# Layer-norm sums: the last k-tile enters TensorE's partition sums as a term of its own

## The chip, the cores and the metric

The kernel runs on one core of a Trainium2 chip. The metric is the device time of one execution in microseconds (us); lower is better. Shown are the median of several executions and one execution that was profiled.

## The reference, cut to what matters

Four layers, each a token mixer (Fourier, attention, pooling, gMLP) and a gated ConvFFN. Every sub-layer normalises twice: the post-norm of the residual sum and, after it, the modulated norm of the next sub-layer.

```python
def _layer_norm(x, g=None, b=None):
    xf = x.astype(F32)
    mu = jnp.mean(xf, axis=-1, keepdims=True)
    var = jnp.mean(jnp.square(xf - mu), axis=-1, keepdims=True)
    y = (xf - mu) * lax.rsqrt(var + LN_EPS)
...
    x_p = _layer_norm(ALPHA * x_p + m_p[2] * y_p, ln_g[i, 0], ln_b[i, 0])
    x_s = _layer_norm(ALPHA * x_s + m_s[2] * y_s, ln_g[i, 0], ln_b[i, 0])
    h_p = _layer_norm(x_p) * (1 + m_p[4]) + m_p[3]
    h_s = _layer_norm(x_s) * (1 + m_s[4]) + m_s[3]
```

The width is 1024 features; 512 sample tokens and 128 prompt tokens run through the same weights.

## The kernel before, in words

The state `x` lies feature-major in SBUF: 8 k-tiles of 128 features (partitions) by 640 tokens. Work on tokens is cut into two halves, `HALVES` 0 and 1 (256 and 384 tokens) or, in two layers, 2 and 3 (384 and 256). A large product is three float32r matmuls for each k-tile (`mm3`, L189 to L191); TensorE (PE) runs these nearly without a break.

A norm needs, for each token, the mean of the values and of the squares over all features, so over 8 k-tiles and 128 partitions. It is done in these steps:

- `sums_add` (L337 to L351) is called for each k-tile as its values come out, either from `evac` (L452, VectorE adds the scaled product to `x`) in `project` and the pooling `mix`, or from `ln1` (L411, L412) in `boundary`. ScalarE squares the tile (L348, tile `lnt`), GpSimd (POOL) adds the values to a running sum (L349, tile `tmp`), and the squares are added to a second running sum (L355) one call later: on POOL where the first norm's sums are built in `project`, on VectorE (DVE) in `boundary` and in `mix`.
- `ln_stats` (L359) adds the last squares on DVE (L355) and has PE sum over the partitions: one float32 matmul of 128x1 for each block of 128 tokens and each of the two sums (L368, tile `st`), with the running sum as the stationary operand and a column of 1/1024 (`onesD`). Then L372 to L376 make the mean and the reciprocal deviation (`lnv`; the power is POOL's), PE broadcasts both over the partitions (L388, tile `bc`), and `centre`, `ln1` and `ln2` (L399, L411, L420) apply them.

`boundary` does this twice for each half. The steps of the first half are handed out between the matmuls of the second (`LN_A`). Those of the second half, the exposed one, lie between the first matmuls of the next stage (`LN_B`, `LN_P`), which run on the first half alone: float32 matmuls (L503) or float32r ones. A scheduler then fixes one instruction order for each engine; engines run in order and wait on semaphores.

There are 30 calls of `ln_stats`, and 150 matmuls of L368.

Of the kernel before, what the change touches and what calls it, by code (L numbers as in the profile page):

```python
# [17 lines left out]
NK = 8  # L18
# [80 lines left out]
def at(d, key):  # L99
    return d.get(key, d[None])  # L100


def steps(g, n):
    for _ in range(n):
        next(g, None)
# [10 lines left out]
class Kern:  # L116
# [206 lines left out]
        return self.mod[L][:, ch, kt, g:g + 1]  # L323


    def sums_new(self, half):

        w = HALVES[half][1] - HALVES[half][0]
        S = types.SimpleNamespace(first=None, last=None, pool=True, nt=w // 128, n=0)
        if w <= 256:  # L330
            t = self.tmp([128, 2, w])
            S.s = (t[:, 0], t[:, 1])
        else:
            S.s = (self.tmp([128, w]), self.tmp([128, w]))
        return S

    def sums_add(self, S, z, t=None, scale=None, bias=None, pool=True):  # L337


        nc = self.nc  # L340
        src, kw = (z, {}) if t is None else (t, dict(scale=scale, bias=bias))
        n, S.n = S.n, S.n + 1
        if n == 0:
            nc.scalar.activation(S.s[1], src, AF.Square, **kw)
            S.first, S.pool = z, pool
            return
        sq = self.small("lnt", [128, z.shape[1]], LNT)
        nc.scalar.activation(sq, src, AF.Square, **kw)  # L348
        nc.gpsimd.tensor_add(S.s[0], z, S.s[0] if n > 1 else S.first)  # L349
        self.sums_end(S)  # L350
        S.last = sq  # L351
# [6 lines left out]
    def ln_stats(self, S, half, eps, together):  # L358


        nc, v = self.nc, self.nc.vector
        a, b = HALVES[half]
        S.pool = False
        self.sums_end(S)
        st = self.st([128, 2, 3])
        for q in range(2):
            for t in range(S.nt):
                nc.tensor.matmul(st[:, q, t:t + 1], S.s[q][:, 128 * t:128 * t + 128], self.onesD, start=True, stop=True)  # L368
        cv = self.small("lnv", [128, 2, 3])
        w = self.small("lnw", [128, 3])  # L370
        n = slice(0, S.nt)
        v.tensor_copy(cv[:, 0, n], st[:, 0, n])  # L372
        nc.scalar.activation(w[:, n], st[:, 0, n], AF.Square)
        v.tensor_sub(w[:, n], st[:, 1, n], w[:, n])
        v.tensor_scalar(out=w[:, n], in0=w[:, n], scalar1=0.0, scalar2=eps, op0=ALU.max, op1=ALU.add)
        nc.gpsimd.tensor_tensor(out=cv[:, 1, n], in0=w[:, n], in1=self.mhalf[:, n], op=ALU.pow)  # L376
        yield
        out = []
        for i in range(2):
            if b - a > 256 or not together:  # L380
                ps = self.bc()
            elif i == 0:
                both = self.bc()
                ps = both[:, 0:256]
            else:
                ps = both[:, 256:512]
            for t in range(S.nt):
                nc.tensor.transpose(ps[:, 128 * t:128 * t + 128], cv[:, i, t:t + 1].to_broadcast([128, 128]), self.ident)  # L388
            out.append(ps[:, 0:b - a])
        yield out  # L390
# [65 lines left out]
    def project(self, gs, units, L, ch, after, fill=None, halves=(0, 1)):  # L456

        ws = {}  # L460
        key = L, ch // 3
        keep = at(KEEP, key)
        sched = list(at(LN_A, key))
        for half in halves:
            S = self.sums_new(half)
            first = half == halves[0]
            a, b = HALVES[half]
            for m in (range(NK) if first else range(NK - 1, -1, -1)):
                if first or m < NK - keep:
                    ws[m] = units(m)  # L470
                ps = self.mm([128, b - a])
                n = len(gs)
                for i in range(n):
                    self.mm3(ps, ws[m](i), (gs[i][:, 0, a:b], gs[i][:, 1, a:b]), i == 0, i == n - 1)
                    while not first and sched and sched[0] <= 8 * (NK - 1 - m) + 8 * i / n:
                        steps(ln, 1)
                        sched.pop(0)
                if first and fill is not None:
                    fill()
                self.evac(ps, L, ch, m, half)  # L480
                self.sums_add(S, self.x[:, m, a:b])
            if first:
                ln = after(half, S)
        steps(ln, 99)
        after(half, S)
# [280 lines left out]
    def boundary(self, L, which, box, pre=None):  # L766

        def ln(half, S):


            together = (L, which) == (2, 0)
            st = self.ln_stats(S, half, EPS_POST, together)
            next(st)
            yield
            MU, R = next(st)
            yield
            if L == DEPTH - 1 and which == 1:
                a, b = HALVES[half]
                for k, t in self.centre(MU, half, AHEAD_L):
                    self.ln1(t, R, L, which, half, k)  # L780
                    self.load(self.a["y"][:, k, a:b], self.x[:, k, a:b])
                    yield
                return
            nL, ch = (L, 3) if which == 0 else (L + 1, 0)
            if half in (0, 2):
                if which == 1 and nL == 2:
                    box["hf"] = [self.act([128, 2, T], F32) for _ in range(NK // 2)]
                else:
                    box["h"] = self.new_h()
                    box["h32"] = self.hlp.tile([128, NK, 256], F32, tag="hl", name=self.nm("h32"))  # L790
            S = self.sums_new(half)
            for k, t in self.centre(MU, half, at(AHEAD, (L, which, half))[0]):
                self.ln1(t, R, L, which, half, k, S)
                yield
            st = self.ln_stats(S, half, EPS, together)
            next(st)
            yield
            MU, R = next(st)
            yield
            for k, t in self.centre(MU, half, at(AHEAD, (L, which, half))[1]):  # L800
                self.ln2(t, R, nL, ch, half, k, box)
                yield

        def after(half, S):
            g = ln(half, S)
            if half in (0, 2):
                return g
            sched = list(LN_P if half == 3 else at(LN_B, (L, which)))
            n = 0
            for i, w in enumerate(pre(box) if pre is not None else ()):  # L810
                n += w
                while sched and sched[0][0] <= n:
                    steps(g, sched.pop(0)[1])
            steps(g, 99)
        return after
# [367 lines left out]
    def pool_pre(self, box):  # L1183

        nc, a = self.nc, self.a
        w = [self.raw_unit(a["wpool"][i], [128, 2, 2, 256]) for i in range(2)]
# [22 lines left out]

        def mix(half):  # L1210
            x0, x1 = HALVES[half]
            S = self.sums_new(half)
            for m in range(NK):
                ps = self.mm([128, x1 - x0])
                nc.tensor.matmul(ps, zero[:, 0:128], zero[:, 0:x1 - x0], start=True, stop=False)
                for t in range(5):
                    lo, hi = BAND_RANGE[t]
                    c0, c1 = max(lo, x0), min(hi, x1)
                    if c0 >= c1:
                        continue  # L1220
                    off = 128 * t - 8
                    nc.tensor.matmul(ps[:, c0 - x0:c1 - x0], u[t][:, 128 * m:128 * m + 128],
                                     band[m // 4][:, (m // 2) % 2, BAND_KIND[t], c0 - off:c1 - off], start=False,
                                     stop=(t == 4 or BAND_RANGE[t + 1][0] >= x1))
                self.evac(ps, 2, 2, m, half, gate)
                self.sums_add(S, self.x[:, m, x0:x1], pool=False)
                yield 2
            return S

        box["pool"] = hw, mix  # L1230
        yield from hw((0, 1, 2))
        S = yield from mix(0)
        for _ in self.after[2, 0](0, S):
            yield 2
# [307 lines left out]
```

## Time and profile before

| | |
|---|---|
| median of 3 runs | 2783.2 us (2778.14 to 2785.08) |
| the profiled execution | 2783.77 us |
| its span in the trace | 2782.0 us |
| PE busy | 2705.3 us, 97% of the span |
| DVE, ACT, POOL busy | 77%, 48%, 16% |
| mean granted clock of PE | 0.987 of full |

The span is the time from the first to the last instruction of the profile. A line of the waits view names the engine that waited, the line and tile it waited for, and the total, the count and the longest. In a timeline, a row is a run of like instructions on one engine: start, length, engine, line, operation, output and inputs, and in brackets the idle time before it and who ended it. A float32 matmul leaves more than one record of each kind (PEld is the load of the stationary operand, PE the product).

### The profile page before, as it was taken

What the parts mean: (1) busy time and instruction counts of PE and PEld (TensorE: products, weight loads), DVE (VectorE), ACT (ScalarE), POOL (GpSimd) and SP (SyncE); (2) the same over time, 40 slices, a digit from 0 to 9 for tenths busy, and PEclk for the clock granted to TensorE, in tenths of its full rate; (3) what the DMA queues carried; (4) which work ended last, traced back from release to release, by engine and by line L of the source; (5) the groups of instructions that cost most, each with busy time, mean ns of one, the idle gap of its engine ahead of it and who ended that gap; (6) DMA issues with size and microseconds to landing.
All of it is one profiled execution on the core that took longest, in us unless ns stands there. A gap on an engine that the chain in (4) does not pass through costs nothing. (4 is left out here: it accounts for less than half of the span.)

```text
span 2782.0 us, 46206 instructions
## 1 busy us (share of the span) xinstructions
PE 2705.3 (97%) x17466; PEld 2583.4 (93%) x17466; DVE 2134.0 (77%) x4636; ACT 1345.6 (48%) x2424; POOL 455.2 (16%) x477
## 2 busy tenths in 40 slices
PE   7999999999999999999999999999999999999998
PEld 3799999999989999999978999989689999999998
DVE  6879987786697887777487778876997858776775
ACT  4656232335576662323366544454632237544563
POOL 1251000015312400000253000014200024000013
PEclk9999999999999999999988999999999999999999
DMA  6735655452312344444203345653453323344462
GB/s 234 252 107 172 199 169 156 159 167 80 113 52 77 107 153 159 149 155 160 90 34 106 107 113 153 163 146 116 150 188 123 124 74 114 99 111 117 122 152 70
DMA packets 110880, 367.84 MB, mean 132 GB/s; under 512 B 12609, under 2 KB 15297, under 8 KB 110529
## 3 DMA queue, kind: packets, MB, share of 16 engines
q1 hardware_dynamic: 102016, 341.28, 38.0%
q0 software_dynamic: 8640, 23.60, 4.8%
q8 instruction: 138, 2.26, 0.3%
q14 instruction: 86, 0.70, 0.1%
HBM read 335.73 MB, written 2.88 MB: 122 GB/s over the span
## 5 line engine op out<-in xcount | busy, mean ns | idle before, releaser
L189 PE MATMUL mm<-act,hl 128*128 128x384 f32 (+3 forms) x4448 | 1383.8, 312 | 11.2 <-ACT lnt L720 8.2
L191 PE MATMUL mm<-act,hl 128*128 128x384 f32 (+3 forms) x4448 | 1379.9, 311 | 8.3 <-DMA hl<-raw 4.3
L190 PE MATMUL mm<-act,hl 128*128 128x384 f32 (+3 forms) x4448 | 1379.4, 310 | 2.4 <-POOL act L434 1.6
L189 PEld LDWEIGHTS mm<-act,hl 128*128 128x128 f32 x4448 | 842.2, 189 | 18.6 <-ACT lnt L720 9.9
L191 PEld LDWEIGHTS mm<-act,hl 128*128 128x128 f32 x4448 | 842.0, 189 | 10.9 <-DMA hl<-raw 5.3
L190 PEld LDWEIGHTS mm<-act,hl 128*128 128x128 f32 x4448 | 842.8, 189 | 5.2 <-POOL act L434 2.6
L174 ACT CAST hl<-raw 128x1024 fp32r<-128x1024 f32 (+4 forms) x449 | 432.9, 969 | 447.7 <-PE mm L191 312.0
L299 DVE SCALAR_TENSOR_TENSOR bc<-raw,cbc 128x512 f32<-128x512 f32 x608 | 406.8, 720 | 112.9 <-DMA raw<-in_wmod 112.7
L179 DVE TENSOR_TENSOR hl<-raw,hl 128x1024 fp32r<-128x1024 f32 (+4 forms) x384 | 455.5, 1191 | 45.2 <-ACT hl L174 42.9
L452 DVE SCALAR_TENSOR_TENSOR x<-mm,mod,x 128x256 f32<-128x256 f32 (+2 forms) x456 | 185.2, 435 | 155.5 <-PE mm L191 154.5
L349 POOL TENSOR_TENSOR tmp<-x,tmp 128x256 f32<-128x256 f32 (+1 forms) x180 | 178.5, 996 | 145.7 <-DVE x L452 100.4
L177 POOL DMA_DIRECT2D hl<-raw x60 | 51.9, 864 | 638.0 <-ACT hl L176 389.7
L545 DVE SCALAR_TENSOR_TENSOR tmp<-ap,vecs,tmp 128x512 f32<-128x512 f32 x232 | 112.7, 547 | 48.4 <-ACT tmp L543 48.2
L558 POOL MEMSET ap<- 128x1 f32 x24 | 2.2, 104 | 842.4 <-DVE tmp L545 373.3
L183 ACT CAST act<-tmp 128x640 fp32r<-128x640 f32 (+1 forms) x125 | 88.8, 710 | 94.5 <-DVE tmp L550 60.4
L399 DVE TENSOR_TENSOR lnt<-x,bc 128x256 f32<-128x256 f32 (+1 forms) x240 | 110.1, 480 | 13.0 <-PE bc L388 12.8
L547 ACT ACTIVATE tmp<-tmp 128x640 f32<-128x640 f32 x58 | 42.9, 740 | 158.2 <-DVE tmp L545 158.2
L348 ACT ACTIVATE lnt<-x 128x256 f32<-128x256 f32 (+1 forms) x112 | 51.2, 466 | 129.4 <-DVE x L452 127.1
L184 DVE TENSOR_TENSOR act<-tmp,act 128x640 fp32r<-128x640 f32 (+1 forms) x125 | 99.9, 799 | 11.0 <-ACT act L183 10.5
L355 DVE TENSOR_TENSOR tmp<-tmp,lnt 128x384 f32<-128x384 f32 (+1 forms) x126 | 94.2, 749 | 13.6 <-ACT lnt L348 12.4
L503 PE MATMUL mm<-h,raw 128*128 128x256 f32 x416 | 101.2, 399 | 1.8 <-DVE lnt L420 1.8
L174 ACT CAST hl<-sums 128x1024 fp32r<-128x1024 f32 x60 | 62.9, 1049 | 77.1 <-PE mm L191 50.8
(267 smaller groups left out, 3687.5 us busy)
## 6 DMA issues: line engine op xcount, KB each, us to landing
raw<-in_wup SPq DMA_DIRECT2D x216, 512.0 KB, 3.6
raw<-in_wmod SPq DMA_DIRECT2D x184, 512.0 KB, 4.0
raw<-in_wdn SPq DMA_DIRECT2D x55, 448.0 KB, 3.7
hl<-raw POOLq DMA_DIRECT2D x30, 512.0 KB, 5.4
raw<-in_wgv SPq DMA_DIRECT2D x24, 512.0 KB, 3.6
raw<-in_wdn SPq DMA_DIRECT2D x23, 512.0 KB, 3.6
raw<-in_wgo SPq DMA_DIRECT2D x19, 512.0 KB, 4.0
raw<-in_wqk SPq DMA_DIRECT2D x18, 512.0 KB, 3.5
```

The costliest lines, as they stand in the source:

```text
L174: nc.scalar.copy(hl[:, 0], r)
L179: (e or nc.vector).tensor_sub(hl[:, 1], r, hl[:, 0])
L184: (e or self.nc.vector).tensor_sub(dst[:, 1], src, dst[:, 0])
L189: t.matmul(out, lhs[0], rhs[0], start=start, stop=False, skip_group_check=on)
L190: t.matmul(out, lhs[0], rhs[1], start=False, stop=False, skip_group_check=on)
L191: t.matmul(out, lhs[1], rhs[0], start=False, stop=stop, skip_group_check=on)
L299: nc.vector.scalar_tensor_tensor(out=self.bc(), in0=r[:, sl], scalar=1.0, in1=self.cbc[:, g, sl], op0=ALU.mult, op1=ALU.mult, accum_out=ac ...
L349: nc.gpsimd.tensor_add(S.s[0], z, S.s[0] if n > 1 else S.first)
L399: self.nc.vector.tensor_sub(t, self.x[:, k, a:b], MU)
L452: nc.vector.scalar_tensor_tensor(out=self.x[:, m, s0:s1], in0=ps[:, s0 - a:s1 - a], scalar=sc, in1=self.x[:, m, s0:s1], op0=ALU.mult, op1= ...
L503: self.nc.tensor.matmul(ps, w[:, k, :], h32[:, k, :], start=k == 0, stop=k == NK - 1)
L545: nc.vector.scalar_tensor_tensor(out=c[:, sl], in0=ap[:, o + i:o + i + n], scalar=cw(i), in1=c[:, sl], op0=ALU.mult, op1=ALU.add)
```

## The change: what it does

In 18 of the 30 calls `sums_new` is made with `direct` set: in `project` for halves 1 and 3, in `boundary` for halves 1 and 3 and for both halves of two boundaries, and in the pooling `mix` for both halves. There, the eighth k-tile's values and squares are not added to the running sums. They are kept as `S.tail`, and `ln_stats` issues a second matmul behind each of L368's (L374 in the changed file), with the tail tile as the stationary operand, accumulating into the same column of `st` (L376). The add of the seventh tile's squares stays where it was.

```diff
-    def sums_new(self, half):
+    def sums_new(self, half, direct=False):
...
-        S = types.SimpleNamespace(first=None, last=None, pool=True, nt=w // 128, n=0)
+        S = types.SimpleNamespace(first=None, last=None, pool=True, nt=w // 128, n=0, direct=direct, tail=None)
...
         nc.scalar.activation(sq, src, AF.Square, **kw)
+        if S.direct and n == NK - 1:
+            self.sums_end(S)
+            S.tail = (z, sq)
+            return
         nc.gpsimd.tensor_add(S.s[0], z, S.s[0] if n > 1 else S.first)
...
-                nc.tensor.matmul(st[:, q, t:t + 1], S.s[q][:, 128 * t:128 * t + 128], self.onesD, start=True, stop=True)
+                sl = slice(128 * t, 128 * t + 128)
+                nc.tensor.matmul(st[:, q, t:t + 1], S.s[q][:, sl], self.onesD, start=True, stop=S.tail is None)
+                if S.tail is not None:
+                    nc.tensor.matmul(st[:, q, t:t + 1], S.tail[q][:, sl], self.onesD, start=False, stop=True)
...
-            S = self.sums_new(half)
+            S = self.sums_new(half, half in (1, 3))
...
-            S = self.sums_new(half)
+            S = self.sums_new(half, half in (1, 3) or (L, which) in ((1, 1), (2, 0)))
...
-            S = self.sums_new(half)
+            S = self.sums_new(half, True)
```

The order changes near these calls. On PE, at the second norm of the second half behind layer 0's ConvFFN, at about 695 us of the trace, before:

```order
L191 MATMUL mm_7169<-act_6605,hl_7129 128x256
L368 MATMUL st_7195<-onesD,tmp_6968 128x1 x3
L368 MATMUL st_7195<-onesD,tmp_6969 128x1 x3
L946 MATMUL mm_7209<-onesH,tmp_7161 128x1 x2
L189 MATMUL mm_7221<-act_6598,hl_7166 128x256
```

and in the changed program:

```order
L191 MATMUL mm_7180<-act_6613,hl_7140 128x256
L374 MATMUL st_7205<-onesD,tmp_6980 128x1
L376 MATMUL st_7205<-onesD,x 128x1
L374 MATMUL st_7205<-onesD,tmp_6980 128x1
L376 MATMUL st_7205<-onesD,x 128x1
L374 MATMUL st_7205<-onesD,tmp_6980 128x1
L376 MATMUL st_7205<-onesD,x 128x1
L374 MATMUL st_7205<-onesD,tmp_6981 128x1
L376 MATMUL st_7205<-onesD,lnt_7038 128x1
L374 MATMUL st_7205<-onesD,tmp_6981 128x1
L376 MATMUL st_7205<-onesD,lnt_7038 128x1
...
L954 MATMUL mm_7225<-onesH,tmp_7172 128x1 x2
```

Six matmuls have become twelve, between the same neighbours. On PE, at the second norm of the second half behind the pooling mixer, at about 1504 us, before:

```order
L503 MATMUL mm_15875<-h_15414,raw_15873 128x256 x6
L368 MATMUL st_15846<-onesD,tmp_15712 128x1 x3
L503 MATMUL mm_15875<-h_15414,raw_15873 128x256 x2
L368 MATMUL st_15846<-onesD,tmp_15713 128x1 x3
L503 MATMUL mm_15892<-h_15414,raw_15890 128x256 x7
L388 MATMUL bc_15900<-identr,lnv_15853 128x128 x3
```

and in the changed program:

```order
L511 MATMUL mm_15919<-h_15448,raw_15917 128x256 x2
L374 MATMUL st_15884<-onesD,tmp_15752 128x1
L511 MATMUL mm_15919<-h_15448,raw_15917 128x256 x2
L376 MATMUL st_15884<-onesD,x 128x1
L374 MATMUL st_15884<-onesD,tmp_15752 128x1
...
L511 MATMUL mm_15919<-h_15448,raw_15917 128x256
L374 MATMUL st_15884<-onesD,tmp_15753 128x1
L376 MATMUL st_15884<-onesD,lnt_15810 128x1
...
L511 MATMUL mm_15919<-h_15448,raw_15917 128x256 x3
L511 MATMUL mm_15936<-h_15448,raw_15934 128x256 x7
L396 MATMUL bc_15944<-identr,lnv_15897 128x128 x3
```

The first sum stands four wide matmuls earlier, and ten instead of seven wide matmuls stand between them and the broadcast. On POOL, at the program's end (the last k-tiles of half 3), before:

```order
L355 TENSOR_TENSOR tmp_28478<-tmp_28478,lnt_28707 128x256
L349 TENSOR_TENSOR tmp_28478<-x,tmp_28478 128x256
L355 TENSOR_TENSOR tmp_28478<-tmp_28478,lnt_28740 128x256
L349 TENSOR_TENSOR tmp_28478<-x,tmp_28478 128x256
L376 TENSOR_TENSOR lnv_28783<-lnw_28784,mhalf 128x2
```

and in the changed program:

```order
L360 TENSOR_TENSOR tmp_28538<-tmp_28538,lnt_28767 128x256
L354 TENSOR_TENSOR tmp_28538<-x,tmp_28538 128x256
L360 TENSOR_TENSOR tmp_28538<-tmp_28538,lnt_28800 128x256
L384 TENSOR_TENSOR lnv_28845<-lnw_28846,mhalf 128x2
```

POOL's last add of values is gone; its last add of squares stays.

## Rows read from the trace of the kernel before

**Rows 1.** Page, part 1: busy time, share of the span, instructions

```profile
PE 2705.3 (97%) x17466; PEld 2583.4 (93%) x17466; DVE 2134.0 (77%) x4636; ACT 1345.6 (48%) x2424; POOL 455.2 (16%) x477
```

**Rows 2.** Waits of PE: total us, times, longest us

```profile
PE st L368 <- POOL tmp L349: 8.5, 8, 2.2
PE bc L388 <- POOL lnv L376: 8.5, 10, 1.4
PE mm L189 <- ACT lnt L720: 8.2, 6, 2.6
PE mm L191 <- DMA hl<-raw: 4.3, 4, 1.3
PE mm L191 <- DVE hl L179: 4.0, 4, 1.9
PE mm L190 <- DVE hl L179: 3.0, 2, 1.6
...
PE st L368 <- DVE tmp L355: 0.8, 1, 0.8
```

**Rows 3.** Instructions of L368: records, ns min/median/max, then the matmuls' own count

```profile
L368 PEld LDWEIGHTS st<-onesD,tmp x300: 186/192/338, 142.4 to 2770.8; 128*128 128x128 f32 x150
```

**Rows 4.** Timeline near 695 us: start us, length us, engine, line

```profile
694.59 0.28 PE L190 MATMUL mm<-act,hl 128*128 128x256 f32 x1
...
694.71 0.28 PE L191 MATMUL mm<-act,hl 128*128 128x256 f32 x1
694.72 1.43 PEld L368 LDWEIGHTS st<-onesD,tmp 128*128 128x128 f32 x12
694.83 1.40 PE L368 MATMUL st<-onesD,tmp 128*128 128x1 f32 x12
```

**Rows 5.** Timeline near 1439 us, PE's loads

```profile
1439.51 0.93 PEld L368 LDWEIGHTS st<-onesD,tmp 128*128 128x128 f32 x4 [0.91 <-DVE tmp L355]
```

**Rows 6.** Windows in layers 1 and 2: stretch, length, busy, then PEclk, DMA

```profile
1403.00:1407.00 4.00, 1.82 (x17) 1.62 (x15) 3.96 (x9) 2.59 (x5) 3.92 (x4) 1.00 0.00 0
1407.00:1414.00 7.00, 7.00 (x36) 6.92 (x35) 3.37 (x10) 0.59 (x2) 5.47 (x7) 0.51 0.69 246
...
1437.50:1451.00 13.50, 10.73 (x34) 8.29 (x35) 11.61 (x33) 6.80 (x19) 4.62 (x8) 0.51 0.00 0
...
1468.50:1478.50 10.00, 8.19 (x25) 6.62 (x25) 8.50 (x23) 6.22 (x13) 3.08 (x4) 0.50 0.00 0
...
1506.00:1513.00 7.00, 7.00 (x22) 5.75 (x21) 2.70 (x5) 2.52 (x4) 1.70 (x1) 0.52 0.46 154
```

**Rows 7.** Timeline of the last norm, from 2767.9 us

```profile
2767.92 0.73 POOL L349 TENSOR_TENSOR tmp<-x,tmp 128x256 f32<-128x256 f32 x1
...
2768.26 0.61 DVE L452 SCALAR_TENSOR_TENSOR x<-mm,mod,x 128x128 f32<-128x128 f32 x2 [1.91 <-PE mm L191]
2768.60 0.73 POOL L355 TENSOR_TENSOR tmp<-tmp,lnt 128x256 f32<-128x256 f32 x1
2768.99 0.42 ACT L348 ACTIVATE lnt<-x 128x256 f32<-128x256 f32 x1 [2.12 <-DVE x L452]
2769.28 0.73 POOL L349 TENSOR_TENSOR tmp<-x,tmp 128x256 f32<-128x256 f32 x1
2769.50 0.79 DVE L355 TENSOR_TENSOR tmp<-tmp,lnt 128x256 f32<-128x256 f32 x1 [0.63 <-ACT lnt L348]
...
2770.07 1.05 PE L368 MATMUL st<-onesD,tmp 128*128 128x1 f32 x8 [1.85 <-POOL tmp L349]
```

**Rows 8.** Timeline near 1504 us, second norm behind the pooling mixer

```profile
1501.19 1.07 POOL L349 TENSOR_TENSOR tmp<-x,tmp 128x384 f32<-128x384 f32 x1 [0.20 <-ACT x L412]
...
1501.97 0.71 ACT L412 ACTIVATE x<-lnt,vecs 128x384 f32<-128x384 f32 x1
...
1502.82 1.38 POOL L349 TENSOR_TENSOR tmp<-x,tmp 128x384 f32<-128x384 f32 x1 [0.56 <-ACT x L412]
...
1504.25 0.83 PE L368 MATMUL st<-onesD,tmp 128*128 128x1 f32 x6 [2.22 <-POOL tmp L349]
```

## The prediction

> **What bounds the kernel now.** I read the page's busy times first: PE is busy 2705 of 2782 us, no other engine over 77% [rows 1]. So what PE has to do is nearly the whole time, and anything added to PE costs its length unless it falls into one of PE's waits. Second the waits of PE, to see what this change could win. PE waits for the sums' inputs 8.5 us for POOL's adds of values and 0.8 us for DVE's adds of squares, in nine waits, the longest 2.2 us; it waits another 8.5 us before the broadcasts, for POOL's power [rows 2]. Third the timelines around the norms, to see what one more sum costs PE and what ends its wait: most of the 18 changed calls look like the one at 695 us, with no wait at all before the sums [rows 4], and a few like those at 1504 and 2770 us, where PE stands 2.22 and 1.85 us for POOL [rows 7, 8]. Last the windows for PE's granted clock, since the sums of layers 1 and 2 lie partly where it is 0.50 to 0.52, the 1.2 GHz level [rows 6].
>
> **What is removed.** 18 adds on POOL and 18 on DVE, 0.73 to 1.38 us each in the rows that show one [rows 7, 8]. Neither engine sets the pace, so they are worth only what PE waits for them: at most 9.3 us [rows 2].
>
> **What is added.** Of the 18 calls, 13 work on 384 tokens (three blocks, two sums: 6 more matmuls) and 5 on 256 (4 more): 78 + 20 = 98 matmuls on PE. Their price stands in the trace. Each of L368's 150 matmuls left two records (300) [rows 3], and in a group the records follow each other at the pace of the loads: 12 loads take 1.43 us, the last of them 0.19, so a step is (1.43 - 0.19) / 11 = 0.113 us, though the product has one column. That is nearly what a 256-column float32r product costs beside it (694.59 to 694.71, 0.12 us) [rows 4]. So one matmul costs PE 2 x 0.113 = 0.225 us, and 98 of them **22.1 us**. The bounds: 98 x 0.119 x 2 = 23.3 if the whole 1.43 us is divided by 12, and 11 us if each matmul stood alone behind a wide one, whose product hides the first of its two loads, as the load that starts at 694.72 lies under the product of 694.71 [rows 4]. In the new order nearly all stand in groups of 6 to 12; some nine are alone between wide matmuls, which takes back 9 x 0.113 = **1.0 us**.
>
> The Trainium skill (FP8 and Floating Point Precision, TensorE Precision Notes) says that true FP32 takes four passes through the array. The trace has two records for each such matmul [rows 3]; if four were paid at a record's price, the added work would be 44 us instead of 22 and the sum 22 us higher. The records, whose time is measured, decide.
>
> At the 1.2 GHz level four loads took 0.93 us, 0.23 each, against 1.43 / 12 = 0.12 [rows 4, 5]. About 16 of the 98 lie in the half-clock windows (both second norms and the pooling mixer's first one) [rows 6]; at 0.11 us more for each of two records, 16 x 2 x 0.11 = **3.5 us** more.
>
> **What comes back.** The wait before the sums goes only as far as the next input is early. At the program's end the last values are in `x` at 2768.87 (2768.26 + 0.61), and the sixth add of values ends at 2768.65; the first sum may start at about 2768.95 instead of 2770.07, 1.1 us of the 1.85 [rows 7]. Late next is POOL's add of squares that stays, which ends at 2769.33, and ScalarE's last square, at 2769.41; four matmuls on the values keep PE until 2769.85, so these cost nothing. The sums then end at 2768.95 + 8 x 0.225 = 2770.75, against 2771.12: the last norm gains 0.4 us net. DVE's add of squares (2769.50 to 2770.29) was already beneath PE's four records on the values. Near 1504 us, `x` is written at 1502.68 (1501.97 + 0.71) and POOL's last remaining add ends at 1502.26, so the sum of values may start at about 1502.75: 1.5 us earlier [rows 8]. But it now takes 12 records where it took 6, and the second sum still waits for DVE's remaining add of squares. Together 2.6 of 4.07 us, 64%; applied to the 9.3 us [rows 2], **5.9 us** come back. The bounds are 0, if the remaining adds are as late, and 9.3.
>
> Behind the sums, the wait for POOL's power (8.5 us, 10 times [rows 2]) begins when the sums end and moves with them; the work between them does not get shorter. The new order puts a wide matmul or more beneath some of these waits. I take **2 us** back, bounds 0 and 5.
>
> New waits: each tail matmul waits for ScalarE's last value or square, and wide matmuls stand behind it in PE's queue. In the first norm these come from `evac` and were waited for anyway (POOL's and DVE's adds needed the same tiles), so no new one is counted. DVE's 18 adds less free it a little earlier for the splits of L179, for which PE waits 7 us elsewhere [rows 2], mostly not near a norm; I take nothing.
>
> **The sum.** 22.1 - 1.0 + 3.5 - 5.9 - 2 = +16.7 us on the profiled execution's 2783.8, so 2800.5. That execution lies 0.6 us above the median of the runs; against the median I forecast **2800 us**, 0.6% slower. With the unknowns at their ends the sum runs from about 7 (11 + 3.5 - 5.9 - 2) to 27 (23.3 + 3.5): 2790 to 2811.
>
> **Rivals.** *The added work is absorbed later.* In parts of layers 2 and 3 other engines hold PE up: ScalarE's L720, the DMA into `hl` and DVE's splits, 19.5 us together [rows 2]. If those engines' work does not move with PE's lateness, PE meets these waits late and they shrink. For it: the waits are there. Against it: ScalarE and DVE work there on what PE produces, so they are late with it. If half is absorbed, +16.7 - 10 = +7: 2790.
>
> *The added products cost less than their loads.* The first load of a group is hidden beneath the product ahead of it [rows 4]; if half of the loads were, the added work is at its lower bound of 11 us and the sum +16.7 - 11 + 1.0 = +7 as well: 2790. Against it: eleven steps of 0.113 us in a row [rows 4]. The Trainium skill (TensorE: Matmul & The Clock Gate, Wait — 56ns, not 53.3ns?) says that starts of small products come no closer than about 25 ns; whoever takes that floor for the price gets, as an estimate, 196 x 0.025 = 4.9 us and no change in the time. The trace agrees that it is a floor, and shows that this group does not reach it.
>
> *The waits were worth more than their length: faster.* The clock falls to the 1.2 GHz level right after PE's waits of 2.18 and 2.22 us (PE busy 1.82 of 4.00 us before 1407, at 1.00; then 0.51) [rows 6, 8]. If, with the last adds gone, PE does not stand still there, the clock may stay at 2.4 GHz in all four windows: 7 + 13.5 + 10 + 7 = 37.5 us at half pace, 19 us won. With all of the 9.3 and of the 8.5 us back: 22.1 - 1.0 - 9.3 - 8.5 - 19 = -16: 2768. It decides when more than 21 us come back. Against it: the two waits shrink by about two thirds at best, what fills them has one column, and 11 of the 18 calls have neither a wait nor a low clock to lose.
>
> *The clock falls at more places.* Each added group keeps PE on one-column products for up to 1.4 us longer. If four of the norms at 1.00 fell to half for 7 us as in rows 6, each would cost 3.5 us: 2814. Against it: the 12 records at 695 us already run at full pace [rows 4].
>
> That the change doesn't do what it says I leave out: the order shows the doubled matmuls and the missing adds.
>
> **How the numbers follow.** The forecast 0.66, absorbed 0.12, cheap products 0.05, faster 0.07, clock lower 0.10. A measurement of this kernel tells about 0.3%, 8.4 us, from no change. Faster by more takes the case of the waits alone, 0.07; within 0.3% lie the absorbed case and the cheap products, 0.17; slower is the forecast and the lower clock, 0.76. The range takes in the forecast's bounds, most of the two cases within 0.3% and a part of the lower clock: 2787 to 2812. It leaves out the faster case, the low ends of those two and the high end of the last.
>
> **What would show it.** PE's busy time up by 15 to 25 us. The records of L374 and L376 together 496 (300 + 196), stepping at 0.113 us in groups. The wait for POOL before the sums down from 8.5 to 3 to 5 us, not gone. The norm at 695 us longer by 1.3 us with nothing behind it shorter. At the end the sums start some 1.1 us earlier after the last product and the tail gains under 0.5 us. I would be wrong if the group's step were far from 0.113 us, if the low-clock windows vanished, or if PE's waits in layers 2 and 3 fell by 10 us.

## The result and the profile after

The changed kernel takes 2798.9 us (median of 6 runs, 2793.9 to 2808.9) against 2781.4 us for the kernel before (6 runs beside it): a ratio of 1.0072 [1.0057, 1.0088], slower by 20 us [16, 24]. Repeated (`after_again` below) it was 1.0054 [1.0039, 1.0069], 15 us [11, 19]. The forecast was 2800 us, or +16.7 us on the profiled execution.

The profiled execution of the changed kernel took 2793.94 us, the shortest of its six; its span of 2792.2 us is only 10.2 us longer than that of before, at the same mean granted clock of 0.987. One execution is not the mean of many: a second profile of the unchanged kernel (`control` below) has PE busy 2697.0 us at 0.989, where the first has 2705.3 us at 0.987. The readings below say which part of the 15 to 20 us this one shows and which it does not.

The page's busy times, which answer to [rows 1]:

```profile
PE 2727.8 (98%) x17662; PEld 2606.4 (93%) x17662; DVE 2116.0 (76%) x4618; ACT 1345.0 (48%) x2424; POOL 434.8 (16%) x459
```

PE is busy 22.5 us longer and has 196 more records: 98 matmuls of two each. POOL and DVE have 18 instructions less each. PE's idle time (span less busy) goes from 76.7 to 64.4 us.

The records of the two lines of sums (engine, operation, count; ns min/median/max; first and last start in us), for [rows 3]:

```profile
L374 PE MATMUL st<-onesD,tmp x300: 164/250/353, 138.4 to 2781.0; 128*128 128x1 f32 x150
```

```profile
L376 PE MATMUL st<-onesD,x x98: 167/250/352, 177.5 to 2780.3; 128*128 128x1 f32 x98
L376 PE MATMUL st<-onesD,lnt x98: 167/250/352, 179.7 to 2781.2; 128*128 128x1 f32 x98
```

300 + 196 = 496, as forecast. The norm of [rows 4], with the record behind the sums in PE's timeline of before, and then PE's timeline of the changed kernel:

```profile
696.09 0.58 PE L946 MATMUL mm<-onesH,tmp 128*128 128x1 f32 x4
```

```profile
695.32 0.28 PE L191 MATMUL mm<-act,hl 128*128 128x256 f32 x1
695.44 0.28 PE L374 MATMUL st<-onesD,tmp 128*128 128x1 f32 x2
695.58 0.36 PE L376 MATMUL st<-onesD,x 128*128 128x1 f32 x2
695.80 0.36 PE L374 MATMUL st<-onesD,tmp 128*128 128x1 f32 x2
...
697.81 0.36 PE L376 MATMUL st<-onesD,lnt 128*128 128x1 f32 x2
698.04 0.58 PE L954 MATMUL mm<-onesH,tmp 128*128 128x1 f32 x4
```

No wait stands before the sums, and 24 records follow each other: from 695.58 to 697.81, 20 records later, are 2.23 us, 0.112 us each. From the group's start to the next product are 2.60 us, where 12 records took 1.26 (694.83 to 696.09): 1.34 us more, as forecast.

PE's waits, for [rows 2]:

```profile
PE mm L189 <- ACT lnt L728: 7.5, 6, 1.7
PE st L374 <- POOL tmp L354: 5.0, 5, 2.4
PE bc L396 <- POOL lnv L384: 4.0, 6, 1.4
PE mm L190 <- DVE hl L179: 2.6, 2, 1.6
PE mm L191 <- DMA hl<-raw: 2.5, 2, 1.3
PE mm L191 <- DVE hl L179: 2.1, 7, 0.5
...
PE st L374 <- DVE lnw L382: 1.0, 1, 1.0
PE bc L396 <- DVE lnv L380: 0.8, 3, 0.3
```

The waits before the sums fall from 9.3 to 6.0 us, but the longest is still there: 2.4 us. The 1.0 us for L382 is a new wait, for DVE; the waits of before have none of the kind. The waits before the broadcasts fall from 9.3 us (8.5 and, in a row not shown ahead, 0.8 for DVE) to 4.8. Those for L728 (L720 before), for the DMA into `hl` and for DVE's splits fall from 19.5 to 14.7.

**Where the longest wait stayed.** The second norm of layer 1's second sub-layer, PE before, then PE and POOL in the changed kernel:

```profile
1406.62 1.15 PE L368 MATMUL st<-onesD,tmp 128*128 128x1 f32 x6 [2.18 <-POOL tmp L349]
```

```profile
1410.43 0.38 PE L374 MATMUL st<-onesD,tmp 128*128 128x1 f32 x2 [2.36 <-POOL tmp L354]
```

```profile
1409.07 2.00 POOL L354 TENSOR_TENSOR tmp<-x,tmp 128x384 f32<-128x384 f32 x2
```

PE stands for POOL's last remaining add of this half (the first of the two in the row) as long as it stood for the removed one: 2.36 us, against 2.18 before. The order of PE tells why: between the sums ahead of these and these, the trace of before has 133 other product records, that of after 120. The scheduler has put the sums 13 records further forward. At the norm of [rows 8] the sums were put forward too, and the wait falls, but by 1.1 us and not the 1.5 forecast, from 2.22 to 1.13:

```profile
1511.78 0.38 PE L374 MATMUL st<-onesD,tmp 128*128 128x1 f32 x2 [1.13 <-POOL tmp L354]
```

**The end.** The last norm, for [rows 7]:

```profile
2779.42 0.72 POOL L360 TENSOR_TENSOR tmp<-tmp,lnt 128x256 f32<-128x256 f32 x1
```

```profile
2779.52 0.38 PE L374 MATMUL st<-onesD,tmp 128*128 128x1 f32 x2 [0.50 <-POOL tmp L354]
...
2781.10 0.36 PE L376 MATMUL st<-onesD,lnt 128*128 128x1 f32 x2
```

Here no wide product of a next stage stands behind the sums, and the wait falls from 1.85 to 0.50 us. The sums last 16 records instead of 8, 0.9 us more, so that about 0.45 us is gained.

**The clock.** Windows of the changed kernel (stretch, length, then busy of PE, PEld, DVE, ACT, POOL, then PEclk), each pair a stretch with a group of 24 records and the one behind it:

```profile
695.40:698.00 2.60, 2.60 (x26) 2.60 (x24) 0.00 (x0) 0.75 (x2) 1.24 (x1) 1.00 0.04 13
699.50:702.90 3.40, 3.40 (x18) 3.40 (x17) 0.00 (x0) 0.00 (x0) 0.68 (x1) 0.50 0.38 140
963.00:965.80 2.80, 2.80 (x26) 2.80 (x27) 1.13 (x3) 1.49 (x3) 0.00 (x0) 0.99 0.75 293
965.80:969.20 3.40, 3.40 (x19) 3.40 (x18) 2.13 (x4) 1.04 (x1) 0.86 (x1) 0.51 0.82 274
1979.00:1982.90 3.90, 3.90 (x28) 3.12 (x26) 3.90 (x11) 3.90 (x11) 0.00 (x0) 1.00 0.52 150
1982.90:1986.30 3.40, 3.40 (x6) 1.56 (x6) 3.29 (x11) 0.93 (x4) 0.88 (x1) 0.50 0.72 292
2358.00:2361.80 3.80, 3.80 (x36) 3.80 (x34) 2.69 (x3) 2.40 (x4) 0.00 (x0) 1.00 0.73 208
2361.80:2368.60 6.80, 6.80 (x33) 6.80 (x34) 2.93 (x7) 2.26 (x3) 0.86 (x1) 0.50 0.75 263
```

PE is busy all the time and the clock at 1.00 (0.99 in one row) while the group runs; at its end, or up to 1.5 us behind it, the granted clock falls to the 1.2 GHz level for 3.4 or 6.8 us. Two more new stretches begin at 180.7 us, behind groups of 8 and 10 records, and at 1959 us, behind one of 24. In the profile of before the norms at these six places run at 1.00. A fall does not follow every such group: three more groups of 24, at 203, 941 and 2330 us, have none behind them, and in the second profile of the changed kernel (`after_again`) only three of the six places have one (699, 966 and 1983 us). On the other side four stretches of before are gone: the one near 1506 us [rows 6], which `after_again` has again at 1512 us, one of 6.8 us near 769, and two of 3.4 us near 144 and 1864. So this one execution has as low a mean clock as the profiled one of before; over all the timed runs the mean granted clock of the changed kernel was 0.9847 (6 runs) and 0.9858 (5), that of the kernel before 0.9886 in the 21 runs beside the latter.

### The profile page after: what moved, and what is told of

It reads as the page before. It is cut to its first block, busy times and chain, and to the rows that moved or that the text cites. A ratio compares the mean times of both kernels' runs of the same rounds, so it can differ in the third digit from the quotient of the medians.

```text
span 2792.2 us, 46536 instructions
## 1 busy us (share of the span) xinstructions
PE 2727.8 (98%) x17662; PEld 2606.4 (93%) x17662; DVE 2116.0 (76%) x4618; ACT 1345.0 (48%) x2424; POOL 434.8 (16%) x459
## 4 chain that ended last, share of the span: by engine, by line
PE 63%; DVE 3%; issue 2%; ACT 2%; DMA 2%; POOL 1%; SPq 0%; POOLq 0%; ACTq 0%; DVEq 0%
PE mm L189 18%; PE mm L191 17%; PE mm L190 17%; PE mm L1298 1%; PE mm L511 1%; DMA hl<-raw 1%; PE bc L189 1%; PE bc L191 1%; PE bc L190 1%; PE st L374 1%; DMA raw<-in_wup 1%; PE mm L1391 1%; PE st L376 1%; ACT x L420 1%; PE mm L1213 0%
## 5 line engine op out<-in xcount | busy, mean ns | idle before, releaser
L354 POOL TENSOR_TENSOR tmp<-x,tmp 128x256 f32<-128x256 f32 (+1 forms) x162 | 157.7, 978 | 114.3 <-DVE x L460 78.4
L184 DVE TENSOR_TENSOR act<-tmp,act 128x640 fp32r<-128x640 f32 (+1 forms) x125 | 99.8, 798 | 10.2 <-ACT act L183 9.8
L420 ACT ACTIVATE x<-lnt,vecs 128x256 f32<-128x256 f32 (+1 forms) x128 | 82.2, 648 | 23.4 <-DVE lnt L419 22.7
```

The lines of the kernel that those rows point to most:

```text
L420: nc.scalar.activation(z, t, AF.Identity, scale=scale, bias=bias)
```

## The experiments

The theory: each added matmul costs two loads of 0.112 us, part of that is taken out of waits, and the rest is the slowdown. The rivals, as they were put to the runs: the loads are cheap and something else is slow; the falling clock carries most of it; the removed adds are worth a lot (or nothing). Differences in us below are (ratio - 1) x 2777, the kernel before's time beside these runs.

**The kernel before, word for word** (`control`). No edit.

> The kernel before, word for word: what the comparison itself shows of no change. All theories: within 0.1% (3 us).

Ratio 0.9999 [0.999, 1.0008]. Its profile, with a span of 2774.6 us, serves below as a second trace of before:

```profile
PE 2697.0 (97%) x17466; PEld 2577.8 (93%) x17466; DVE 2133.3 (77%) x4636; ACT 1345.2 (48%) x2424; POOL 458.7 (17%) x477
```

**The matmuls without their gain** (`price`). The kernel before, with a second matmul behind each of the 18 calls' sums, which multiplies the running sum by a column of zeros; all adds stay.

```diff
+        self.zeroD = cp.tile([128, 1], F32, name="zeroD")
...
-                nc.tensor.matmul(st[:, q, t:t + 1], S.s[q][:, 128 * t:128 * t + 128], self.onesD, start=True, stop=True)
+                sl = slice(128 * t, 128 * t + 128)
+                nc.tensor.matmul(st[:, q, t:t + 1], S.s[q][:, sl], self.onesD, start=True, stop=not S.direct)
+                if S.direct:
+                    nc.tensor.matmul(st[:, q, t:t + 1], S.s[q][:, sl], self.zeroD, start=False, stop=True)
```

> Before with 98 more partition-sum matmuls at the 18 changed calls, against a column of zeros, and all adds kept: the matmuls alone. Theory A (each added matmul costs PE two loads of 0.113 us, and the long groups let the clock fall at some places): 22 us for the matmuls and 5 to 12 us for the clock, 25 to 33 us slower than before. Rival B (the matmuls hide and the change is slow because PE waits for ScalarE's last tile): under 10 us slower.

1.0091 [1.0076, 1.0106]: +25 us [21, 29], with a mean clock of 0.985. Its page:

```profile
PE 2730.7 (97%) x17662; PEld 2608.4 (93%) x17662; DVE 2134.2 (76%) x4637; ACT 1346.3 (48%) x2424; POOL 456.7 (16%) x477
```

and two pairs of its windows around long groups:

```profile
694.00:697.00 3.00, 3.00 (x28) 3.00 (x28) 0.87 (x5) 0.51 (x3) 0.46 (x2) 1.00 0.12 22
697.00:700.40 3.40, 3.40 (x19) 3.40 (x17) 0.05 (x1) 0.00 (x0) 0.77 (x1) 0.50 0.41 140
939.00:942.80 3.80, 3.80 (x30) 3.67 (x30) 1.87 (x8) 0.47 (x2) 0.00 (x0) 1.00 0.66 259
942.80:946.20 3.40, 3.40 (x13) 2.85 (x12) 1.55 (x4) 1.31 (x2) 0.86 (x1) 0.50 0.35 86
```

So the added matmuls alone make the whole slowdown (15 to 20 us) or more, and they bring falls of the clock with them, with every add kept and the waits for POOL before the sums nearly as they were (8.0 us against 8.5).

**The gain without its matmuls** (`drop`). The changed kernel without the line that keeps the tail: the eighth k-tile is neither added nor multiplied in the 18 calls, so their sums run over seven of eight tiles.

```diff
         if S.direct and n == NK - 1:
             self.sums_end(S)
-            S.tail = (z, sq)
             return
```

> The change without its second matmuls: the last k-tile is left out of both sums at the 18 calls, so only the adds go. Theory A: 4 to 9 us faster than before, from PE's waits before the sums and no further; the waits for POOL before the sums fall below 5 us. Rival C (the adds' waits also cost the clock and the waits behind them): 15 us faster or more, with fewer low-clock windows in layers 1 and 2.

1.0020 [1.0008, 1.0031]: 6 us slower, where 4 to 9 us faster was expected. Its wait for POOL before the sums is not shorter but longer than the control's 8.5 us:

```profile
PE st L373 <- POOL tmp L353: 10.9, 8, 4.9
```

PE's timeline and POOL's at the longest of them:

```profile
2344.31 1.44 PE L373 MATMUL st<-onesD,tmp 128*128 128x1 f32 x6 [4.92 <-POOL tmp L353]
```

```profile
2338.54 5.71 POOL L353 TENSOR_TENSOR tmp<-x,tmp 128x384 f32<-128x384 f32 x4 [0.15 <-ACT x L419]
```

```profile
2341.70:2348.50 6.80, 4.19 (x19) 4.19 (x20) 6.80 (x7) 3.82 (x8) 2.48 (x2) 0.50 0.44 149
```

The same sums in the control start at 2344.63 without a wait, with 193 other product records between them and the sums ahead; here there are 152. The scheduler has moved the sums forward by 41 records, further than the missing add makes POOL early. PE then stands 4.9 us, and the clock falls. This chain is read from the trace; the missing adds under PE's old order were not tried, so how much of the 6 us it makes is open. Over the whole profile PE's idle time is only 1.2 us above the control's, and the mean granted clock of the runs is 0.9881 against 0.9888.

**The same change with 64 equal columns** (`after_wide`). The matmuls of the sums write 64 columns instead of one, all alike; only the first is read.

```diff
-        self.onesD = cp.tile([128, 1], F32, name="onesD")
+        self.onesD = cp.tile([128, 64], F32, name="onesD")
...
-        st = self.st([128, 2, 3])
+        st = self.st([128, 2, 3, 64])
...
```

> The change with the column of 1/1024 widened to 64 equal columns (all sums come out 64 times; column 0 is used). Theory A (steps are paced by the loads, 0.113 us; the clock falls behind the long groups of one-column products): the groups keep their step, the new low-clock places outside the pooling layer vanish, 7 to 13 us slower than before instead of 17. Rival D (the falls belong to the waits, not to the products): 15 to 20 us slower, the same low-clock places. Rival E (64 columns lengthen the step): over 20 us slower, step above 0.113 us.

1.0035 [1.0022, 1.0048]: +10 us, with a mean clock of 0.992. Windows that begin with the same four groups of 24 and reach past them:

```profile
700.40:707.00 6.60, 6.60 (x59) 6.60 (x59) 0.99 (x6) 1.66 (x6) 2.12 (x2) 1.00 0.29 87
964.80:972.00 7.20, 6.51 (x57) 6.29 (x55) 4.87 (x10) 4.61 (x7) 0.76 (x1) 1.00 0.89 300
1978.70:1986.00 7.30, 7.30 (x36) 4.77 (x35) 6.35 (x18) 3.48 (x11) 0.89 (x1) 1.00 0.71 230
2355.60:2366.00 10.40, 8.95 (x76) 8.54 (x75) 8.33 (x16) 6.75 (x13) 0.86 (x1) 1.00 0.71 247
```

Inside the groups the step stays at 0.111 to 0.112 us, so it does not depend on whether the product has 64 columns or one; what is left to set it, as far as these runs show, is the load of each record. But the clock stays at 1.00 behind them. The time is 5 to 10 us below that of the changed kernel. Part of that is the falls, but the wider tile changes the order too: PE is busy 10.9 to 14.6 us less than in the two profiles of the changed kernel and idle some 8 us more.

A count over all fourteen profiles bears the falls out. Taken are groups of sums' records that start at 1.00 and have PE idle for less than 0.5 us from 4 us ahead to the group's end, and a fall counts if it begins between the group's start and 2 us behind its end. Of 25 groups of 24 one-column records 14 have one, of 52 groups of 12 none; of 13 groups of 24 records with 64 columns none.

**The zeros with 64 columns** (`price_wide`). The edit of `price` and that of `after_wide` together.

```diff
+        self.zeroD = cp.tile([128, 64], F32, name="zeroD")
...
-                nc.tensor.matmul(st[:, q, t:t + 1], S.s[q][:, 128 * t:128 * t + 128], self.onesD, start=True, stop=True)
+                sl = slice(128 * t, 128 * t + 128)
+                nc.tensor.matmul(st[:, q, t, :], S.s[q][:, sl], self.onesD, start=True, stop=not S.direct)
+                if S.direct:
+                    nc.tensor.matmul(st[:, q, t, :], S.s[q][:, sl], self.zeroD, start=False, stop=True)
```

> The kernel before with 98 more matmuls against zeros, all with 64 columns. The one-column form of it was 25 us slower than before, the 64-column form without the added matmuls 5.6 us slower. Theory A (22 us are the loads, the rest the clock): 24 to 30 us slower than before with hardly a low-clock window outside the pooling layer. Rival I (much of the 25 us was the clock): under 20 us.

1.0058 [1.0046, 1.007]: +16 us [13, 19]. Its page and the stretch that was at half clock in `price`:

```profile
PE 2719.9 (97%) x17662; PEld 2599.5 (93%) x17662; DVE 2135.5 (76%) x4637; ACT 1346.7 (48%) x2424; POOL 453.7 (16%) x477
```

```profile
697.00:704.00 7.00, 7.00 (x62) 7.00 (x62) 3.52 (x11) 1.63 (x6) 0.86 (x1) 1.00 0.26 76
```

Less than the 24 to 30 us expected, so the rival, that much of the 25 us was the clock, is borne out. PE is busy 10.8 us less than in `price`, and the mean granted clock of the runs is 0.991 against 0.985. Of the 25 us, some 9 are the clock's, if the 64 columns change nothing else; the next run shows that they do.

**The kernel before with 64 columns** (`before_wide`). The edit of `after_wide` on the kernel before.

```diff
-        self.onesD = cp.tile([128, 1], F32, name="onesD")
+        self.onesD = cp.tile([128, 64], F32, name="onesD")
...
```

> The kernel before with the same 64 columns. Theory A: its groups are half as long and follow a wait in most low-clock places, so 0 to 5 us faster, the pooling mixer's low-clock window shorter. Rival D: no change, within 3 us. Rival E: 3 us slower or more.

1.0020 [1.0011, 1.0029]: 6 us slower, where 0 to 5 us faster was expected, and this at a higher mean clock (0.991 against 0.989). Its page, at a span of 2782.5 us:

```profile
PE 2699.3 (97%) x17466; PEld 2576.9 (93%) x17466; DVE 2135.6 (77%) x4636; ACT 1344.7 (48%) x2424; POOL 453.4 (16%) x477
```

PE is idle 83.2 us (span less busy) against 77.6 in the control, and its waits are spread over many lines. Why is open: the wider tile changes the order as well, and that was not taken apart. Against this kernel, `price_wide` has 20.6 us more PE work and 10.4 us less idle time. Against it too, and on the same chip, `after_wide` is 5 us slower (2787.7 against 2782.8): with 64 columns in both kernels the change costs a third or less of what it costs with one.

**Half of the calls each** (`first_only`, `second_only`). The first keeps `direct` in `project` and `mix` alone (48 of the 98 matmuls), the second in `boundary` alone (50).

```diff
-            S = self.sums_new(half, half in (1, 3) or (L, which) in ((1, 1), (2, 0)))
+            S = self.sums_new(half)
```

> The change at the nine calls of the first norms alone (project and the pooling mix): 48 of the 98 matmuls. Theory A (the price is each matmul's loads and the clock behind long groups): 7 to 11 us slower, about half of the change. Rival F (the second norms carry the loss, since their sums lie between matmuls of the next stage, while the first norms' fill a wait): 0 to 4 us slower.

1.0059 [1.0045, 1.0072]: +16 us, above the 7 to 11 expected. Its three groups of 24 records, at 935, 1959 and 2331 us, all have a fall to 0.50 behind them, and the mean granted clock of its runs is 0.9872 against 0.9886 for the kernel before.

```diff
-            S = self.sums_new(half, half in (1, 3))
+            S = self.sums_new(half)
...
-            S = self.sums_new(half, True)
+            S = self.sums_new(half)
```

> The change at the nine calls of the second norms alone (boundary): 50 of the 98 matmuls. Theory A (each matmul costs its loads wherever it stands): 6 to 12 us slower. Rival G (the first norms alone were as slow as the whole change, so the second norms' matmuls fill waits or shorten a chain that PE waits for): within 4 us of before.

1.0043 [1.0026, 1.006]: +12 us, in the range. The two make 28 us together, where the whole change has 15 to 20. The parts do not add. Each kernel has an order of its own, and PE's idle time falls by 2.1 and 5.8 us in their profiles against 12.6 in that of the whole change; why so little was not taken apart.

**Three calls only** (`three`). The change at the three calls with the longest waits, 16 matmuls: two boundaries and the last norm.

```diff
-            S = self.sums_new(half, half in (1, 3))
+            S = self.sums_new(half, half == 3 and key == (3, 1))
...
-            S = self.sums_new(half, half in (1, 3) or (L, which) in ((1, 1), (2, 0)))
+            S = self.sums_new(half, (L, which, half) in ((1, 1, 2), (2, 0, 1)))
...
-            S = self.sums_new(half, True)
+            S = self.sums_new(half)
```

> The change at three calls alone, those before which PE stood longest (2.18, 2.22 and 1.85 us): 16 matmuls, 3.6 us. Theory A: 2.5 to 4 us of waits come back, so within 3 us of before. Rival C (a wait taken away also gives the clock back): 4 to 8 us faster, the low-clock windows at about 1407 and 1506 us gone.

1.0029 [1.002, 1.0038]: 8 us slower, where no difference beyond 3 us was expected. The first of the three calls in the control and in `three`, then the other two in `three`:

```profile
1402.37 0.83 PE L368 MATMUL st<-onesD,tmp 128*128 128x1 f32 x6 [2.19 <-POOL tmp L349]
```

```profile
1405.28 0.38 PE L374 MATMUL st<-onesD,tmp 128*128 128x1 f32 x2 [2.35 <-POOL tmp L354]
```

```profile
1505.35 0.38 PE L374 MATMUL st<-onesD,tmp 128*128 128x1 f32 x2 [1.58 <-POOL tmp L354]
```

```profile
2766.61 0.38 PE L374 MATMUL st<-onesD,tmp 128*128 128x1 f32 x2 [0.48 <-POOL tmp L354]
```

The wait of the first call is as long as before, with 120 records ahead of it instead of 133: the change bought nothing there even where it should have bought most. The second waits 1.58 us (control: 2.24), the last norm 0.48 (control: 1.85). The 16 matmuls at 0.225 us are 3.6 us of the 8; the mean granted clock of the runs is 0.9869 against 0.9886, so the clock has a part in the rest, which was not taken apart.

**The tail for the values alone** (`values`). The 18 adds on POOL go, the squares keep DVE's add, 49 matmuls are added.

```diff
-            S.tail = (z, sq)
+            S.last = sq
+            S.tail = (z,)
...
-                if S.tail is not None:
+                if S.tail is not None and q == 0:
```

> The change for the values alone: the tail of the squares is added on DVE as before, so 49 matmuls are added and 18 adds on POOL removed. Theory A (PE's waits are for POOL's adds of values, so half the price buys nearly all that comes back): 4 to 9 us slower. Rival H (what comes back comes from DVE's adds, or from nothing but the order): 11 us slower or more.

1.0024 [1.0012, 1.0035]: +7 us [3, 10], in the range. Half of the matmuls leave about half of the slowdown, or less.

**Both restrictions** (`three_values`). The values alone, at the three calls: 8 matmuls.

```diff
-            S.tail = (z, sq)
+            S.last = sq
+            S.tail = (z,)
...
-            S = self.sums_new(half, True)
+            S = self.sums_new(half)
```

> The change at the three calls before which PE stood longest, and there for the values alone: 8 matmuls, 1.8 us. Theory A with all of the waits' gain (2.5 to 4 us) kept: 2 us faster to 1 us slower. Rival J (the three calls were 8 us slower because the sums are put earlier into PE's order and PE stands for POOL again, and the clock falls as before): 3 to 8 us slower, the longest wait for POOL before the sums still above 2 us.

0.9991 [0.998, 1.0002]: 2.5 us faster, which the interval does not tell from nothing. It is the fastest of the versions tried, and no gain that can be claimed.

**The changed kernel again** (`after_again`). No edit; on the chip of the control.

> The changed kernel again, beside its parts. All theories: 15 to 22 us slower than before.

1.0054 [1.0039, 1.0069]: +15 us. Its profile:

```profile
PE 2724.1 (98%) x17662; PEld 2605.6 (93%) x17662; DVE 2113.6 (76%) x4618; ACT 1345.3 (48%) x2424; POOL 428.9 (15%) x459
```

Against the control's, it has 27.1 us more PE work (2724.1 against 2697.0) and 12.6 us less idle time, a span of 2789.1 against 2774.6.

## Why the prediction was right, and in which terms it was not

The sign, the size (+15 to +20 us measured, +16.7 forecast) and the chief cause, two loads for each added matmul on the engine that sets the pace, were right. Two of the signs that the prediction named came out at or near the edge: the wait for POOL before the sums fell to 5.0 us (forecast 3 to 5), PE's busy time rose by 22.5 us, and by 27.1 in the repeat (forecast 15 to 25). Term by term:

- **The added loads, 22.1 - 1.0 us.** Right as work on PE: 196 more records at 0.112 us make 22.0 us, and `price_wide` has 20.6 us more PE work than `before_wide`, at the same mean granted clock (0.991 in the runs of both). The deduction for lone matmuls was right in kind: where a group follows a wide product, its first record stands only 0.026 to 0.030 us ahead of the next in the trace of after, since its load lies beneath that product. Right as well is that the product's width is not the price: 64 columns keep the step. The Trainium skill (TensorE: Matmul & The Clock Gate, LDWEIGHTS) puts a load at its columns divided by 1.2, in ns, which gives 107 for 128 columns as an estimate; the step in this trace is near it, 111 to 112.
- **The clock, +3.5 us: too small.** The prediction counted the matmuls that lie where the clock was low already, and kept "the clock falls at more places" as a rival at a tenth, for "the 12 records at 695 us already run at full pace". That step failed: the 24 at 695 us run at full pace too, and the clock falls behind them. With 64 columns in their place it does not fall, and the time is 5 to 10 us lower (`after` and `after_again` against `after_wide`) and 9 us lower (`price` against `price_wide`), though not by the clock alone, since those kernels have other orders. The mean granted clock of the runs is 0.003 (`after_again`, same chip) to 0.004 lower, which over 2795 us is 8 to 11 us at most, as an estimate. The profiles show less: PE's added busy time beyond the 22.0 us of loads is 0.5 us (after) and 5.1 us (repeated). The rival's mechanism is therefore part of the result, but not as it was priced: at six places in one profile and three in the other, 3.4 to 6.8 us each at half pace, so 1.7 to 3.4 us lost at a place and not 3.5, while other low stretches went away.
- **What comes back, 5.9 + 2 us: too small, and in other places.** The profiles show 12.3 us (after) and 12.6 us (repeated) less idle time. The sums' waits give 3.3 of the 5.9 us forecast: the scheduler spends the earliness by moving the sums forward, so the longest wait stays as it was (2.36 us) and the fraction of 64%, taken from a fixed order, did not hold. The prediction counted no new wait, and one of 1.0 us is there (L382). The broadcasts' waits give 4.5 us in place of 2, and 4.8 us come from the waits for L728, the DMA into `hl` and DVE's splits. The last would be the rival "absorbed later", at half the size of its condition; but the repeated profile has only 0.9 us of it against the control, so it is not shown. Not all of what came back is owed to the adds that are gone: `price`, which removes none, has 5.4 us less idle time than the control, and `price_wide` 10.4 less than `before_wide`.
- **The end, 0.4 us net gain.** Right: the wait falls by 1.35 us and the sums are 0.9 us longer. Of the three places read here it is the one where the wait fell by all that was forecast; at [rows 8] it fell by 1.1 of 1.5 us, at 1410 us not at all.
- **The removed adds.** That they are worth at most what PE waits for them was right, and still too kind: `drop` removes them without adding a matmul and is 6 us slower, `three` keeps the places where they should pay and is 8 us slower.

That the total came so close is partly luck, for two errors offset each other: the repeated profile has 27.1 us more PE work where the terms for loads and clock made 24.6, and 12.6 us less idle time where 7.9 were taken. Of what would have proved it wrong, none happened in full: the step was 0.112 us, not all low-clock stretches vanished, and the later waits fell by 4.8 and 0.9 us, not 10. The second item of that list should have asked for new ones.

Open is what the order alone does. `drop`, `before_wide` and `three` are each at least 4 us slower than their added matmuls explain, and each has a PE order of its own. The granted clock is a part of it in `three` and at most 2 us in `drop`, and it goes the other way in `before_wide`. No run held the order fixed.

## What to carry to other kernels

In this kernel an add on an idle engine was cheaper than a matmul on the engine that sets the pace, however narrow its product: 98 float32 matmuls of one column cost what their 196 loads cost. Count the load records of a trace, not the columns. Before a shortened dependency is priced by the waits of the old trace, look at the new order, for a scheduler may turn the earliness into an earlier start of the same wait. Where a change makes a run of narrow products longer, read the granted clock of the stretch behind the run, not only of the run itself.

## What the runs showed that was not expected

- The granted clock falls to 1.2 GHz behind 14 of 25 groups of 24 one-column float32 records with PE idle for less than 0.5 us around them (at 695 us: busy 2.60 of 2.60 us at 1.00, then 0.50), and behind none of 52 groups of 12. The Trainium skill (TensorE: Matmul & The Clock Gate, HAM oscillation) tells of pauses of PE as what lowers the clock. The trace has falls behind waits too, those of 2.18 and 2.22 us [rows 6, 8], but in the rows at 695 us it shows no pause. With 64 equal columns, the same step and the same loads, the clock stayed at 1.00 behind all 13 such groups. Why the narrow products do this, and why not every time, is open.
- Those 64 columns raised the mean clock of the changed kernel from 0.985 to 0.992 and came with 5 to 10 us less, though all but one column of each product go unread; on the kernel before they came with 6 us more.
